# A two-layer diffusion block: where twelve modulation pairs of the first layer are placed, and how much room attention asks for

## The chip, the cores and the metric

The kernel runs on one core of a Trainium2 chip. TensorE (PE) does the matrix products, VectorE (DVE), ScalarE (ACT) and GpSimd (POOL) the elementwise work, and SyncE (SP) issues all DMA transfers from one queue, in order. The metric is the device time of one execution in microseconds (us); lower is better.

## The reference, cut to what matters

The program computes two layers of a block that works on 512 latent tokens and 256 context tokens of width 1024. All values are float32.

```
for i in range(2):
    mod_l = split(silu(c) @ mod_w[i] + mod_b[i], 6)       # six modulation vectors, latent
    mod_c = split(silu(c_ctx) @ mod_w[i] + mod_b[i], 6)   # the same for the context
    h_l = rms_norm(x, g) * (1 + mod_l[1]) + mod_l[0]      # and h_c
    pa, pb, pc, pd = split(h @ w_in[i])                   # projections of four mixers
    o = concat(rwkv7(pa), diff_attention(pb), gla(pc), gqa(pd))
    x = x + mod_l[2] * (o @ w_out[i])
    x = x + mod_l[5] * conv_ffn(modulate(x, g2, mod_l[3], mod_l[4]), ...)
    # the context xc takes the same path in the first layer
```

Parts 0 and 1 of the modulation are needed ahead of the projections. Parts 2, 3 and 4 are needed only when all four mixers are done: part 2 at the output projection, parts 3 and 4 at the norm after it. These three parts are 24 vectors of 128 channels in the first layer, and the kernel works them out in twelve pairs. They are the pairs of this change.

## The kernel before, in words

**Streams on a planned clock.** Each piece of work is a Python generator that issues instructions and then yields a planned duration in planned nanoseconds. `weave` (line 305) keeps a planned clock for each stream and always advances the stream whose clock is lowest; so the yields set the order in which instructions are issued, and no yield is a measured time. An engine takes its instructions in an order close to that one: the framework below may let a few later instructions of the same engine pass while one waits, as the trace shows at the modulation pairs. Below, "plan 192" means 192 thousand planned nanoseconds after the start of a layer's mixing stage.

**The mixing stage** of a layer weaves `rwkv`, `gla`, `attentions` and `projections`, and in the first layer `mod_mix`. `projections` (line 776) multiplies the normed input by eighteen blocks of `w_in`: eleven feature blocks of 7,776 planned ns each in the first layer and seven token blocks of six tiles of 2,640. Each block sets a flag for its consumer: `da ready` comes after eleven feature blocks and five token blocks, `gq ready` after all of them. Then it gives back the input (eight slabs), the weight ring (four) and the staging ring. `attentions` waits for `da ready` and then, in `begin` (line 1074), until a number of whole slabs is free (`room`, line 871). `rwkv` makes features for two directions, two passes each (`front`, line 1517, with `features` from line 1417); each pass waits until nine half slabs and two whole ones are free (`halves`). Direction 0 then inverts small blocks in a long row of VectorE steps (lines 1492 and 1494) and starts its chain of chunks (`rw_prep`, `rw_chain`), each of which asks for seven whole slabs; direction 1 does the same after its own features.

**On-chip buffers** come from an arena of 30 slabs of 1,536 float32 columns, cut into 24 grains of 64. A slab holds one kind of data (plain float32, or the rounded form that the split-precision matmuls read). A buffer that breaks a whole slab pays a price in `find`, and buffers of a third of a slab are put at the thirds.

**A modulation pair** (`mod_pair`, line 465) loads 1 MB of weights, issues eight matmuls of 32 by 256 columns in four column strips (line 470, two recorded passes each), a ScalarE copy out of PSUM (line 472), two small matmuls that sum the strips (line 474) and a VectorE add (line 477). `mod_mix` (line 521) issues the twelve later pairs. It has three buffers of 1,024 columns, loads each pair in two halves of 512 KB, uses the buffers in turn, takes a PSUM bank of the first four, and yields 16,000 after each pair. Attention and the projections use the same four banks.

**Split-precision weights** (`weights`, line 367): each weight tile is loaded to the staging ring (line 376), rounded by ScalarE (line 382), and the rest is taken by GpSimd (line 383); three matmuls per tile follow (lines 392 for features, 770 for tokens). In attention, keys and queries are rotated (lines 917 to 924), split (936, 937), transposed on TensorE (432), and then come scores (1012, 1015), the maximum (1018), the exponential (1020) and the values (1048).

Of the kernel before, what the change touches and what calls it, by code (L numbers as in the profile page):

```python
# [223 lines left out]
class Net:  # L224
# [293 lines left out]
        self.free(first, ms, r, t1, t2, rb, ps)  # L518
        return rs

    def mod_mix(self, dt):

        ws = [self.new([4, 256]) for _ in range(3)]
        e = 0
        for i in range(KD, len(MODP)):
            w = []
            for q in range(2):
                self.nc.sync.dma_start(out=ws[e % 3], in_=self.A["modp"][i][:, 4 * q:4 * q + 4])
                w += [ws[e % 3][:, k] for k in range(4)]
                e += 1  # L530
            ps = yield from self.bank(1, 0, 4)
            self.mod_pair(i, w, ps)
            self.free(ps)
            yield dt
        self.free(*ws, self.c32)
# [425 lines left out]
    def attentions(self, li, S):  # L961
# [10 lines left out]
        def keys(g):  # L972
            hd, nh = g.hd, P // g.hd
            for t in range(NT):
                raw = load(g, "k", t, g.hp * P, P)
                y = self.rope(raw, t, nh, hd, g.ktab, g.C["kr"][:, t, g.hp * nh:g.hp * nh + nh])
                s = self.new([4, P], F32R)
                if g.da:
                    self.split_stack(s.rearrange("p h (c d) -> p h c d", c=4), y, "HLHL", 4, 32)
                else:  # L980
                    sv = s.rearrange("p (e h) (c d) -> p e h c d", e=2, c=2)
                    yb = y.unsqueeze(2).to_broadcast([P, 2, 2, 64])
                    nc.scalar.copy(out=sv[:, 0], in_=yb)
                    nc.vector.tensor_tensor(out=sv[:, 1], in0=yb, in1=sv[:, 0].bitcast(F32), op=ALU.subtract)
                yield from self.transpose4(s, g.kst[t // 3][:, :, t % 3 * P:(t % 3 + 1) * P], 0, self.AB)
                self.free(s, raw)
                yield 1200
# [86 lines left out]
        def begin(kind, hp, before):  # L1074

            g = SimpleNamespace(kind=kind, hp=hp, da=kind == "da", hd=32 if kind == "da" else 64, qs={})
            yield from self.wait(S, kind + " ready")
            if before is None:
                yield from self.room(5)
            g.C = S[kind]  # L1080
            if hp:
                g.ktab, g.qtab, g.nlam, g.lam_init = before.ktab, before.qtab, before.nlam, before.lam_init
            else:
                g.ktab = self.rope_tables(kind, g.hd, self.rw[kind + "k"], 1.0)
                g.qtab = self.rope_tables(kind, g.hd, self.rw[kind + "q"], g.hd ** -0.5)
                if g.da:
                    g.nlam, g.lam_init = self.diff_lambda(li)
            g.kst = [self.new([4, hb], F32R) for _ in range(2)]
            g.vs = self.new([NT, 2, 64])
            nc.sync.dma_start(out=g.vs.rearrange("p t h d -> p t (h d)"),  # L1090
                              in_=self.raws["da", "v"][:, :, hp * P:hp * P + P] if g.da else self.raws["gq", "k"][:, :, P:2 * P])
            yield from keys(g)
            g.oT = [self.new([T]) for _ in range(1 if g.da else 2)]
            g.units = []
            for t in range(nt):
                g.units += [(t, hi) for hi in range(0, 2 if g.da else 4, 2)]
            return g
# [21 lines left out]
        parts = (("da", 0), ("da", 1), ("gq", 0))  # L1119
        ready, late, ends = [], None, []  # L1120
        nxt = yield from begin(*parts[0], None)
        for i in range(len(parts)):
            g = nxt
            for t, hi in g.units:
                if t not in g.qs:
                    yield from self.room(self.ROOM[li][3])
                    yield from queries(g, t)
                for h in (hi, hi + 1):
                    yield from self.room(self.ROOM[li][3])
                    got = yield from scores(g, t, h)  # L1130
                    if late is not None:
                        ready.append(late[:3] + (combine(late[0], *late[3]),))
                    late = (g, t, hi, got)
                    if len(ready) == 2:
                        yield from pair(ready, ends)
                        ready = []
                if (t, hi) == g.units[-1] or g.units[g.units.index((t, hi)) + 1][0] != t:
                    self.free(g.qs.pop(t))
            self.free(*g.kst)
            if i + 1 < len(parts):  # L1140
                yield from self.room(self.ROOM[li][2])
                nxt = yield from begin(*parts[i + 1], g)
            if i + 1 == len(parts) or parts[i + 1][1] == 0:
                self.free(g.ktab[3], g.qtab[3])
# [711 lines left out]
    def run(self):  # L1856
# [28 lines left out]
        def last(li, S):  # L1885
            x, hf, spans = [], [], self.spans(li < L - 1)
            parts, sts = [[q] for q in spans], [{}, {}]
            yield from self.w_out(li, od, xd[li], x, sts)
            yield from self.norm(li, "nfg", x, sts, hf, parts)
            S["normed"] = True  # L1890
            sts = [{}, {}]

            def done(m, i, a, b):
                if li < L - 1:
                    nc.sync.dma_start(out=xd[1][:, m, a:b], in_=x[m][:, a:b])
                    self.squares(x, m, a, b, sts[i])
                else:
                    nc.sync.dma_start(out=self.out[:, m, a:b], in_=x[m][:, a:b])

            yield from self.ffn(li, x, hf, done, S)  # L1900
            if li < L - 1:
                self.rings(4, 3)
                yield from self.norm(li + 1, "nmg", x, sts, h, parts)
            else:
                self.free(*x)
# [4 lines left out]
        for li in range(L):  # L1910
            self.load_rows(li)
            self.arena.BREAK = 100
            self.AB, S = 4, {}
            streams = [self.rwkv(li, S, od), self.gla(li, S, od), self.attentions(li, S), self.projections(li, h, S)]
            if li == 0:
                streams.append(self.mod_mix(16000))
            self.weave(*streams, pace=self.PACE[li][:1] + self.PACE[li][2:])
            self.rings(4, 3)
            h = []
            streams = [last(li, S)]  # L1920
            self.arena.BREAK = 40
            if li < L - 1:
                streams.append(self.ffn_mod(S))
            else:
                S["ffn gate"] = True
            self.weave(*streams)
# [19 lines left out]
```

## Time and profile before

| what | value |
|---|---|
| median of 3 runs | 2382.31 us (2373.57 to 2385.05) |
| the profiled execution | 2371.69 us, its span 2369.8 us |
| mean granted TensorE clock | 0.954 of full speed |
| TensorE busy | 2194.0 us (93%) |
| VectorE busy | 1327.0 us (56%) |
| twelve later pairs, first weights issued | 37.8 us |
| twelve later pairs, last weights issued | 329.6 us |

Busy times say how long an engine had an instruction running; since matmuls overlap and their ends are modelled, a full TensorE row means that it was never without work, not that it ran at its peak. The granted clock is 1.00 at the upper of two levels (2.4 GHz) and 0.50 at the lower one (1.2 GHz), averaged over a stretch. "Idle before" an instruction names the engine whose result it waited for.

### The profile page before, as it was taken

To read this page: it belongs to the slowest core of one execution; us is meant where nothing else is said; L and a number is where in the kernel's file an instruction comes from. 1 tells how busy PE (TensorE), PEld (TensorE's weight loads), DVE (VectorE), ACT (ScalarE), POOL (GpSimd) and SP (SyncE) were. 2 spreads that over 40 slices of the span, in tenths; PEclk is the share of its full clock that TensorE was granted. 3 is DMA by queue.
4 is the path that set the end of the run, shared out by engine and by line. 5 is a ranking of instruction groups with operands and counts; after the bars stand their busy time and mean duration, and the time that the engine had idled before them with its cause. 6 is when DMAs were issued, how large, how long until landed. Compare 5 with 4: busy or idle time off the path is not lost. (4 is left out here: it accounts for less than half of the span.)

```text
span 2369.8 us, 40603 instructions
## 1 busy us (share of the span) xinstructions
PE 2194.0 (93%) x15656; PEld 1852.1 (78%) x15656; DVE 1327.0 (56%) x2900; ACT 934.2 (39%) x1730; POOL 995.9 (42%) x999
## 2 busy tenths in 40 slices
PE   7989996889989999999999989995899979999999
PEld 3877786768768788888888877785778868888888
DVE  3143567878864696765445643378877565332323
ACT  3333222555564422322223443332465544433333
POOL 1433437123422344434434634455443224555556
PEclk7999997889999999999999989997889989999999
DMA  8322354433234243343333521144233242333334
GB/s 324 116 72 82 102 150 108 105 89 93 58 123 143 82 137 116 109 142 106 116 107 107 172 65 55 59 126 132 69 98 87 77 138 72 102 94 99 98 98 134
DMA packets 241265, 258.51 MB, mean 109 GB/s; under 512 B 102896, under 2 KB 186160, under 8 KB 241072
## 3 DMA queue, kind: packets, MB, share of 16 engines
q1 hardware_dynamic: 241072, 255.92, 36.1%
q8 instruction: 123, 2.02, 0.4%
q14 instruction: 70, 0.57, 0.1%
HBM read 209.69 MB, written 37.77 MB: 104 GB/s over the span
## 5 line engine op out<-in xcount | busy, mean ns | idle before, releaser
L392 PE MATMUL pst<-slab,slab 128*128 128x512 f32 (+1 forms) x6552 | 1236.5, 350 | 14.4 <-POOL slab L650 5.8
L392 PEld LDWEIGHTS pst<-slab,slab 128*128 128x128 f32 x6552 | 1049.6, 190 | 195.8 <-issue 11.3
L383 POOL TENSOR_TENSOR slab<-slab,slab 128x512 fp32r<-128x512 f32 (+1 forms) x428 | 563.7, 1326 | 661.1 <-ACT slab L382 621.3
L382 ACT CAST slab<-slab 128x512 fp32r<-128x512 f32 (+1 forms) x428 | 258.7, 612 | 592.3 <-PE pst L392 418.6
L770 PE MATMUL pst<-slab,slab 128*128 128x256 f32 (+1 forms) x1872 | 254.1, 295 | 9.3 <-POOL slab L383 8.0
L770 PEld LDWEIGHTS pst<-slab,slab 128*128 128x128 f32 x1872 | 242.4, 199 | 20.4 <-POOL slab L383 9.5
L432 PE MATMUL pst<-cst,slab 128*128 128x128 f32 (+1 forms) x968 | 166.4, 305 | 69.1 <-DVE slab L937 21.7
L683 DVE SCALAR_TENSOR_TENSOR slab<-pst,pp,slab 128x511 f32<-128x511 f32 x66 | 41.6, 658 | 299.2 <-ACT slab L680 299.2
L432 PEld LDWEIGHTS pst<-cst,slab 128*128 128x128 f32 (+1 forms) x968 | 120.6, 153 | 96.6 <-DVE slab L937 24.3
L1620 PE MATMUL pst<-slab,slab 128*128 128x128 f32 (+4 forms) x1320 | 160.8, 283 | 7.3 <-DVE slab L1646 3.4
L1620 PEld LDWEIGHTS pst<-slab,slab 128*128 128x128 f32 (+3 forms) x1320 | 132.3, 179 | 29.6 <-issue 14.6
L714 DVE SCALAR_TENSOR_TENSOR slab<-pst,fgate,slab 128x512 f32<-128x512 f32 (+1 forms) x144 | 88.2, 628 | 104.9 <-PE pst L392 104.7
L1020 ACT ACTIVATE slab<-pst,mx 128x768 f32<-128x768 f32 (+1 forms) x120 | 97.7, 815 | 67.6 <-DVE mx L1018 64.3
L1018 DVE TENSOR_REDUCE mx<-pst 128x1 f32<-128x768 f32 (+1 forms) x120 | 100.2, 846 | 35.6 <-PE pst L1012 20.1
L695 POOL TENSOR_TENSOR slab<-slab,slab 128x768 fp32r<-128x768 f32 (+1 forms) x44 | 73.9, 1680 | 70.2 <-ACT slab L694 70.2
L551 DVE SCALAR_TENSOR_TENSOR slab<-slab,slab 128x512 bf16<-128x512 f32 x104 | 92.2, 886 | 5.1 <-DMA slab<-in_modw_dram 3.5
L1048 PE MATMUL pst<-slab,slab 128*64 128x128 f32 x832 | 67.0, 290 | 5.0 <-DVE slab L429 2.9
L1031 ACT ACTIVATE slab<-slab,r 128x768 f32<-128x768 f32 (+1 forms) x80 | 67.7, 852 | 10.0 <-DVE r L1030 9.3
L689 ACT ACTIVATE slab<-slab 128x768 f32<-128x768 f32 (+1 forms) x44 | 32.4, 737 | 85.7 <-DVE slab L685 85.6
L694 ACT CAST slab<-slab 128x768 fp32r<-128x768 f32 (+1 forms) x44 | 32.1, 729 | 85.0 <-DVE slab L691 84.9
L1012 PE MATMUL pst<-slab,slab 128*128 128x384 f32 (+1 forms) x144 | 48.8, 407 | 14.0 <-ACT slab L1020 6.4
L1048 PEld LDWEIGHTS pst<-slab,slab 128*64 128x64 f32 x832 | 46.9, 141 | 18.1 <-DVE slab L429 6.3
(320 smaller groups left out, 2626.6 us busy)
## 6 DMA issues: line engine op xcount, KB each, us to landing
slab<-in_wup_dram SPq DMA_DIRECT2D x88, 512.0 KB, 3.7
slab<-in_modw_dram SPq DMA_DIRECT2D x112, 256.0 KB, 3.0
slab<-in_wdn_dram SPq DMA_DIRECT2D x48, 512.0 KB, 3.5
slab<-in_win_dram SPq DMA_DIRECT2D x46, 512.0 KB, 3.9
slab<-in_modp_dram SPq DMA_DIRECT2D x40, 512.0 KB, 7.0
slab<-in_wout_dram SPq DMA_DIRECT2D x16, 512.0 KB, 3.7
slab<-in_xT_dram SPq DMA_DIRECT2D x16, 384.0 KB, 5.3
slab<-kb SPq DMA_DIRECT2D x24, 256.0 KB, 3.0
```

The costliest lines, as they stand in the source:

```text
L382: nc.scalar.copy(out=w[0], in_=st[:, k:k + q])
L383: nc.gpsimd.tensor_tensor(out=w[1], in0=st[:, k:k + q], in1=w[0].bitcast(F32), op=ALU.subtract)
L392: self.nc.tensor.matmul(ps[:, a:b], w[i][k][:, cols], x[j][k][:, a:b], start=(k == 0 and q == 0), stop=(k == nk - 1 and q == 2))
L432: self.nc.tensor.transpose(out, a.bitcast(F32) if a.dtype != F32 else a, self.c["ident"])
L551: self.tc.keep_in_program_order(nc.vector.scalar_tensor_tensor(out=junk, in0=w, scalar=1.0, in1=self.sc[s][e], op0=ALU.mult, op1=ALU.mult, ...
L695: nc.gpsimd.tensor_tensor(out=HL[:, 1, :n], in0=th[:, :n], in1=HL[:, 0, :n].bitcast(F32), op=ALU.subtract)
L714: nc.vector.scalar_tensor_tensor(out=x[m][:, a:b], in0=ps[:, a:b], scalar=gate[:, m, s:s + 1], in1=x[m][:, a:b], op0=ALU.mult, op1=ALU.add)
L770: self.nc.tensor.matmul(ps[:, :n], h[i][k][:, t * P:(t + 1) * P], w[j][k], start=(k == 0 and q == 0), stop=(k == KD - 1 and q == 2))
L1018: nc.vector.tensor_reduce(out=mx, in_=sv, axis=AX.XY, op=ALU.max, negate=True)
L1020: nc.scalar.activation(out=p[m][:, a:].rearrange("p (e c) -> p e c", e=2 - a // hb), in_=sv, func=AF.Exp, bias=mx, accum_out=lsum[:, m:m + 1])
L1048: nc.tensor.matmul(acc[64 * e:64 * e + 64, :P], vs[e][:, i + j], aT[:, 256 * j + P * e:256 * j + P * e + P], start=(first and j == 0), sto ...
L1620: mm = lambda o, a, b, pos: nc.tensor.matmul(o, a, b, start=True, stop=True, tile_position=pos)
```

## The change

`mod_mix` waits for the flag `gq ready`, which the projections set after their last block. It takes twelve buffers of 512 columns (a third of a slab each, four slabs in all) in place of three of 1,024. A pair's weights come in four DMAs of 256 KB in place of two of 512 KB, so 48 in all in place of 24, and three pairs fit in the buffers at once. After each pair it yields 4,000 in place of 16,000. The buffer `c32`, which holds the condition vector, stays in use until the last pair, as before. Attention's first `begin` of a layer asks for six whole slabs in place of five; this holds in both layers. The pairs themselves, `mod_pair`, are as they were.

```
-    def mod_mix(self, dt):
+    def mod_mix(self, S, dt):
-        ws = [self.new([4, 256]) for _ in range(3)]
-        e = 0
+        n = 12
+        yield from self.wait(S, "gq ready")
+        ws = [self.new([2, 256]) for _ in range(n)]
         for i in range(KD, len(MODP)):
             w = []
-            for q in range(2):
-                self.nc.sync.dma_start(out=ws[e % 3], in_=self.A["modp"][i][:, 4 * q:4 * q + 4])
-                w += [ws[e % 3][:, k] for k in range(4)]
-                e += 1
+            for q in range(4):
+                t = ws[(4 * i + q) % n]
+                self.nc.sync.dma_start(out=t, in_=self.A["modp"][i][:, 2 * q:2 * q + 2])
+                w += [t[:, k] for k in range(2)]
             ps = yield from self.bank(1, 0, 4)
             self.mod_pair(i, w, ps)
             self.free(ps)
...
             if before is None:
-                yield from self.room(5)
+                yield from self.room(6)
...
             if li == 0:
-                streams.append(self.mod_mix(16000))
+                streams.append(self.mod_mix(S, 4000))
```

## Rows read from the trace of the kernel before

**Rows 1.** The page's first part: TensorE's busy time, share of the span, instructions.
```profile
PE 2194.0 (93%) x15656; PEld 1852.1 (78%) x15656; DVE 1327.0 (56%) x2900; ACT 934.2 (39%) x1730; POOL 995.9 (42%) x999
```

**Rows 2.** Windows (us): length, busy us per engine, clock, DMA share, GB/s.
```profile
80.00:340.00 260.00, 246.42 (x2128) 211.25 (x2127) 100.38 (x219) 79.19 (x138) 106.60 (x100) 0.96 0.35 107
340.00:440.00 100.00, 76.48 (x612) 65.03 (x611) 80.83 (x190) 32.81 (x66) 47.34 (x68) 0.83 0.38 98
440.00:560.00 120.00, 105.21 (x930) 85.85 (x930) 93.82 (x236) 66.48 (x145) 33.22 (x62) 0.89 0.36 91
560.00:680.00 120.00, 110.48 (x1123) 91.40 (x1123) 98.25 (x294) 64.45 (x143) 45.70 (x76) 0.95 0.27 73
...
1600.00:1680.00 80.00, 48.69 (x319) 43.87 (x318) 67.52 (x179) 25.01 (x50) 37.02 (x60) 0.74 0.38 105
```

**Rows 3.** Timeline of TensorE after the projections: start, length, line, [idle before].
```profile
390.74 1.11 PE L432 MATMUL pst<-cst,slab 128*128 128x128 f32 x4 [4.86 <-DVE slab L937]
397.08 3.03 PE L432 MATMUL pst<-cst,slab 128*128 128x128 f32 x13 [3.41 <-DVE slab L937]
410.29 3.61 PE L1620 MATMUL pst<-slab,slab 128*64 128x128 f32 x24 [3.01 <-DVE slab L1646]
...
726.19 24.12 PE L392 MATMUL pst<-slab,slab 128*128 128x512 f32 x131
```

**Rows 4.** Timeline of TensorE round one modulation pair.
```profile
308.87 1.07 PE L470 MATMUL pst<-slab,slab 128*32 128x256 f32 x16
309.87 0.74 PE L770 MATMUL pst<-slab,slab 128*128 128x256 f32 x4
310.44 0.59 PE L474 MATMUL pst<-cst,slab 128*128 128x2 f32 x4
310.90 2.63 PE L770 MATMUL pst<-slab,slab 128*128 128x256 f32 x20
```

**Rows 5.** Timeline at the two pairs that stalled TensorE.
```profile
283.64 1.02 PE L474 MATMUL pst<-cst,slab 128*128 128x2 f32 x4 [2.91 <-ACT slab L472]
355.48 0.84 ACT L1430 ACTIVATE slab<-slab 128x768 f32<-128x768 f32 x1 [6.58 <-DVE slab L1428]
356.90 1.02 PE L474 MATMUL pst<-cst,slab 128*128 128x2 f32 x4 [4.27 <-ACT slab L472]
```

**Rows 6.** Waits: SP's queue to 345 us, TensorE over the span (total us, times, longest).
```profile
SPq L528 <- PE pst L470: 35.4, 9, 9.6
...
PE pst L770 <- POOL slab L383: 8.0, 6, 3.0
```

**Rows 7.** Timeline of TensorE: rwkv's feature matmuls, first layer, then second.
```profile
297.27 2.85 PE L1424 MATMUL pst<-slab,lora 64*128 64x512 f32 x8
...
345.07 2.85 PE L1424 MATMUL pst<-slab,lora 64*128 64x512 f32 x8
...
1563.83 2.85 PE L1424 MATMUL pst<-slab,lora 64*128 64x512 f32 x8
...
1579.72 2.84 PE L1424 MATMUL pst<-slab,lora 64*128 64x512 f32 x8
```

**Rows 8.** Windows, VectorE alone: length, busy us, clock, DMA share, GB/s.
```profile
299.70:310.40 10.70, 7.43 (x8) 1.00 0.67 201
311.60:327.50 15.90, 1.67 (x6) 1.00 0.92 256
```

**Rows 9.** Waits of TensorE for ScalarE over the span: total us, times, longest.
```profile
PE pst L432 <- ACT slab L1020: 11.3, 16, 2.3
PE pst L474 <- ACT slab L472: 10.8, 10, 4.3
```

**Rows 10.** DMA issues (count, KB each, us to landing); a window of all engines.
```profile
slab<-in_modw_dram SPq DMA_DIRECT2D x112, 256.0 KB, 3.0
...
slab<-in_modp_dram SPq DMA_DIRECT2D x40, 512.0 KB, 7.0
...
20.00:40.00 20.00, 16.17 (x110) 8.09 (x111) 8.69 (x24) 5.17 (x12) 5.16 (x4) 0.51 1.03 405
```

## The prediction

> **What bounds the kernel now.** I read the page first: TensorE is busy for 93% of the span [rows 1], so the question is where it is not. The windows by stage answer that [rows 2]. From 80 to 340 us, in the first layer's projections, TensorE is busy 246.4 of 260 us, while VectorE has 100.4 and GpSimd 106.6: this stretch is bound by TensorE, and whatever leaves its queue there shortens it. From 340 to 440 us, where the projections end and attention and rwkv start, TensorE is idle for 23.5 of 100 us at a granted clock of 0.83, and VectorE is busy for 80.8. From 440 to 560 us it is idle for 14.8 of 120 us, VectorE at 93.8; from 560 to 680 us for 9.5. So the mixers' stretch is a chain over several engines, with VectorE the fullest. The timeline shows the same in single gaps: TensorE sits idle 4.86, 3.41 and 3.01 us for VectorE's results at 391, 397 and 410 us [rows 3]. The next stage's matmuls start at 726 us [rows 3]; attention is the last mixer before it.
>
> **The pairs leave the projections.** One pair costs TensorE 1.00 us for the eight strip matmuls (308.87 to 309.87) and 0.46 us for the sums (310.44 to 310.90), 1.46 us in all; other matmuls fill the time of the copy [rows 4]. Two of the twelve pairs run ahead of 80 us, where TensorE also waits for the norm; I give those nothing. Ten pairs by 1.46 us are 14.6 us. Two pairs stalled TensorE, because ScalarE's copy came late: 2.91 us and 4.27 us [rows 5]. In the second case ScalarE itself had stood 6.58 us behind a VectorE scan. These 7.2 us go with the pairs. What is late next is the projections' own weights, for which TensorE waited 8.0 us over the whole run in six waits [rows 6]; so I take 5.0 of the 7.2 (bounds 0 and 7.2). SP's queue stood 35.4 us before the twelve pairs' loads, since a buffer was still being read [rows 6]; weights queue behind them. They arrived in time all the same, so I take nothing for it (at most the 8.0 us of TensorE's waits for weights, which cover both layers). Sum of the removal: -19.6 us.
>
> **The pairs come into the mixers' stretch.** Twelve pairs by 1.46 us are 17.5 us of TensorE's time. By the yields of the code the projections end at plan 196 (eleven blocks of 7,776 and 42 tiles of 2,640), and the pairs take 48 from there. Attention's last yield falls at plan 392. The last 196 of the plan take from 386 us (390.74 less 4.86) to 726 us [rows 3], 1.73 us each, so the pairs are spread over some 83 us from the projections' end on. That stretch has TensorE idle for 38.3 of 220 us (340 to 560). Each pair also makes TensorE, which runs its queue in order, wait for ScalarE's copy; behind the waiting matmuls are scores, transposes and rwkv's blocks, and VectorE and ScalarE wait for those. The trace of before has one pair in this stretch, the last, and it waited 4.27 us [rows 5]. The nearest wait of the same engines that is met often there, a transpose behind an exponential, is 11.3 us in 16 waits, 0.7 us each; the pairs' own waits were 10.8 us in 10, with a longest of 4.3 [rows 9]. I take the common wait, 0.7 us, since the one pair stood behind a scan that ends with the features: twelve waits add 8.4 us. Bounds: nothing, if all of it falls into idle time, and 12 x (1.46 + 4.27) = 69 us, if each pair waits like the worst and nothing hides it. Work that TensorE gets into its gaps is free, work ahead of a chain step is not; with 17% of TensorE's time idle here and VectorE at 79%, I take half of 17.5 + 8.4 us: +13.0 us. The pair's one short copy on ScalarE and one short add on VectorE lie in this.
>
> **The loads.** Twelve pairs bring 12 x 1.05 MB. SP issues 24 more DMAs. The first twelve need buffers that the projections gave back, so SP may stand there until the last weights are rounded; behind it are attention's and rwkv's loads, for which there is no row, between nothing and the 35.4 us that SP stood at such loads before [rows 6]. After that a load of pair i+3 waits for pair i's matmuls, and what is queued behind it is used after pair i anyway: I take nothing, the pairs being three deep. Traffic from 340 to 440 us is 98 GB/s [rows 2]; the most that a stretch shows is 405 GB/s [rows 10]. The difference, 307 GB/s, loads a pair in 3.4 us, against 4 plan units or 6.9 us from pair to pair: the loads keep up, at no cost.
>
> In the trace a 256 KB load lands after 3.0 us and one of 512 KB after 7.0 us [rows 10], so here the smaller one is not dearer by the byte. The Trainium skill (DMA: Bandwidth & Descriptors, section Bandwidth) asks for transfers of at least 1 MiB for three quarters of the peak, and its section Anatomy of one DMA puts a constant of about 2.0 us on each. An estimate by that page: 24 more transfers by 2.0 us are 48 us, which would be paid only one after another.
>
> **What the three buffers free.** Until the projections end, `mod_mix` holds no slab any more; its three buffers had each taken two thirds of one. In the first layer the features' third pass follows the second after 47.8 us (297.27 to 345.07), in the second layer, which has no such pairs, after 15.9 us (1563.83 to 1579.72) [rows 7]. The pass asks for nine halves; with three more whole slabs, six halves, it can start right behind the second pass, some 30 us earlier. VectorE's work for a pass is 7.43 us in eight instructions; and from 311.6 to 327.5 us VectorE is busy for only 1.67 of 15.9 us [rows 8]. So one pass goes wholly into idle time, and the fourth, which follows it, in part. Both leave the stretch where TensorE waits for VectorE. I take 1.5 passes: -11.1 us; bounds 0 (other VectorE work is late in their place) and -14.9 us (both passes). The second layer speaks for care: there the passes come early, and yet TensorE is idle for 31.3 of 80 us from 1600 us on [rows 2].
>
> **Six slabs.** In the plan attention may start at 164.7 (`da ready`), but in the kernel before its five slabs come free only when `mod_mix` ends, at 192 of the projections' 196.4. Now six must be free, and the third and fourth pass compete for them. If they come only with the projections' end, attention starts 4.4 plan units or 7.6 us later; if the passes end early, it starts up to 10 units or 17 us sooner. I take 0 between these ends. In the second layer six slabs are free by the allocator's count when five are asked for, so I expect no change there.
>
> **The sum.** -19.6 + 13.0 - 11.1 = -17.7 us. Against the profiled execution (2369.8 us of span, 1.9 us round it, 2371.7 us) that is 2354 us. This execution was 10.6 us under the median of the runs shown, 2382.3 us; applied to the median the sum gives 2364.6, and I predict 2364 us, or 0.8% less.
>
> **Rivals.** (B) All fits into gaps: the pairs cost nothing, both stalls and both passes count: -14.6 - 7.2 - 14.9 = -36.7, 2346 us. For it: 38.3 us of idle time in the right place. Against it: TensorE's queue is in order, and its gaps are not where the pairs stand. (C) Paid back: the passes' place is taken by other VectorE work, and the pairs' 17.5 us lie in full on the chain: -19.6 + 17.5 = -2, 2380 us. For it: the second layer's 31.3 us. (D) Slower: every pair holds TensorE for ScalarE's copy, because ScalarE stands behind VectorE's maximum, as at 356.9 us. At 2.91 us, the smaller of the two stalls [rows 5], with nothing hidden: 12 x 4.37 = 52.4 us, less 30.7, +22, 2404 us. It decides from 30.7/12 = 2.6 us per pair on the chain. For it: one PSUM bank of attention's four is held meanwhile. Against it: of the pairs' ten waits, the other eight share 3.6 us. (E) The loads come one behind the other: 4 x 3.0 = 12 us a pair, 5.1 us over the 6.9 that it has; TensorE waits for each: 12 x (1.46 + 5.1) - 30.7 = +48, 2430 us. That is what the page's constant would make of it; twelve buffers in flight speak against it. (F) The six slabs come late, and the change does not let attention start sooner: -17.7 + 7.6 = -10, 2372 us.
>
> **How the numbers follow.** Forecast 38%, B 17%, C 22%, D 13%, E 3%, F 7%. A measurement of this kernel tells about 0.5% from no change, 12 us: faster means under 2370, slower over 2394 us. Faster: 34% of the forecast's 38, B's 17, 2 of C and 3 of F, 56%. Same: 4 of the forecast, 19 of C, 4 of F, 2 of D, 29%. Slower: 1 of C, 11 of D, E's 3, 15%. The forecast's own range is 2353 to 2375 us. For 8 in 10 the range reaches into B to 2342 and into D to 2400 us.
>
> **What would show it.** No line 470 between 80 us and the projections' end, and the projections' last matmuls (before: done at 386 us) some 20 us earlier; the third group of line 1424 close behind the second; twelve pairs in the 83 us after the projections, with waits of line 474 for line 472 under 1 us (over 2.6 us each: D); less idle time after the projections and a higher granted clock there; no waits of line 470 for its loads (E). If the projections shorten and the stretch up to the output projection grows by as much, C is right.

## The result, and the profile after

The changed kernel takes 2396.91 us (median of 5 runs, 2392.24 to 2407.45); the kernel before takes 2380.74 us in the same comparison. The ratio is 1.0083, with a 95% interval from 1.0055 to 1.0111: slower by 13 to 26 us. The forecast was 2364 us. The profiled execution of the changed kernel took 2396.91 us, its span 2395.1 us, 25.3 us more than the profiled execution before.

In the changed kernel, lines behind `mod_mix` have a number that is higher by one (770 is now 771). The page's first line of busy times and the windows of the same stretches as in [rows 1, 2]:

```profile
PE 2200.2 (92%) x15656; PEld 1852.8 (77%) x15656; DVE 1337.9 (56%) x2900; ACT 934.4 (39%) x1730; POOL 1005.8 (42%) x999
```

```profile
80.00:340.00 260.00, 236.18 (x2038) 205.20 (x2036) 124.48 (x263) 83.40 (x140) 120.37 (x111) 0.96 0.28 83
340.00:440.00 100.00, 74.94 (x571) 60.91 (x571) 75.07 (x203) 32.69 (x70) 38.23 (x59) 0.79 0.46 129
440.00:560.00 120.00, 107.21 (x1026) 82.97 (x1025) 72.98 (x178) 60.45 (x137) 28.81 (x55) 0.96 0.51 141
560.00:680.00 120.00, 111.89 (x1164) 93.68 (x1163) 93.86 (x266) 62.19 (x140) 44.89 (x78) 0.96 0.25 65
1600.00:1680.00 80.00, 52.87 (x443) 47.70 (x442) 58.19 (x132) 17.68 (x38) 38.26 (x48) 0.78 0.51 132
```

VectorE's work has moved: 124.5 us in the projections (100.4 before), 73.0 us between 440 and 560 us (93.8 before). But TensorE's 246.4 us in the projections' window became 236.2 us. With the pairs gone, the matmuls behind them should have moved up and kept it full; instead it ran dry. The timeline of TensorE shows where, behind the four groups of rwkv's feature matmuls (line 1425, as in [rows 7]):

```profile
249.73 2.85 PE L1425 MATMUL pst<-slab,lora 64*128 64x512 f32 x8
276.01 2.85 PE L1425 MATMUL pst<-slab,lora 64*128 64x512 f32 x8
294.41 2.84 PE L1425 MATMUL pst<-slab,lora 64*128 64x512 f32 x8
318.60 2.84 PE L1425 MATMUL pst<-slab,lora 64*128 64x512 f32 x8
...
340.71 1.56 PE L1466 MATMUL pst<-slab,slab 64*64 64x64 f32 x48 [13.20 <-DVE slab L1444]
350.70 4.86 PE L1548 MATMUL pst<-rk,slab 128*128 128x2 f32 x22 [8.43 <-POOL slab L1455]
359.02 3.16 PE L432 MATMUL pst<-cst,slab 128*128 128x128 f32 x12 [3.46 <-DVE slab L938]
361.83 0.56 PE L771 MATMUL pst<-slab,slab 128*128 128x256 f32 x1
...
731.43 0.62 PE L392 MATMUL pst<-slab,slab 128*128 128x512 f32 x2 [0.78 <-ACT slab L1811]
```

The third pass follows the second after 18.4 us (47.8 before), about as forecast. Then the blocks of the fourth pass, the bonus and attention's first transposes stand in TensorE's queue ahead of the projections' last block, and TensorE waits 25 us for VectorE and GpSimd. The projections' last matmul ends at 395 us (386 before); the output projection starts at 731.4 us (726.2 before). The pairs stand between 395 and 511 us, and the waits that the prediction spoke of are small. Waits of TensorE and of SP's queue over the whole span, and the DMA issues:

```profile
PE pst L474 <- ACT slab L472: 3.5, 7, 0.5
PE pst L470 <- DMA slab<-in_modp_dram: 1.8, 3, 1.2
...
SPq L530 <- PE pst L1548: 7.6, 1, 7.6
SPq L530 <- PE pst L470: 5.9, 2, 5.7
...
slab<-in_modp_dram SPq DMA_DIRECT2D x48, 256.0 KB, 4.1
```

All of the 3.5 us and 1.2 of the 1.8 us lie before 80 us, at the eight pairs of the first parts, which use the same lines and which the change leaves alone. From 395 to 731 us line 474 has no wait on TensorE's row, and line 470 has these:

```profile
PE pst L470 <- ACT slab L1021: 2.2, 1, 2.2
PE pst L470 <- DMA slab<-in_modp_dram: 0.6, 2, 0.5
```

In the second layer, where no pair stands and the change only asks for a sixth slab, TensorE's timeline has rwkv's chunks (line 1621) first, and attention's first scores (line 1013) only 44 us later; before, the scores came first (second fence, the kernel before):

```profile
1646.75 1.16 PE L1621 MATMUL pst<-slab,slab 64*128 64x64 f32 x16
...
1690.56 0.62 PE L1013 MATMUL pst<-slab,slab 128*128 128x384 f32 x2
```

```profile
1656.90 0.97 PE L1012 MATMUL pst<-slab,slab 128*128 128x384 f32 x4 [0.73 <-ACT slab L427]
...
1660.75 1.97 PE L1620 MATMUL pst<-slab 64*128 64x64 f32 x8
```

From the second layer's first projection matmul of a token block (line 771) to its first output-projection matmul the trace has 590.2 us (568.8 before). So of the 25.3 us, 5.2 lie in the first layer up to the output projection, 21.4 in this stretch, and -1.3 in the rest.

### The profile page after: what moved, and what is told of

Same layout as the page of the kernel before. It is cut to its first block, busy times and chain, and to the rows that moved or that the text cites. A ratio compares the mean times of both kernels' runs of the same rounds, so it can differ in the third digit from the quotient of the medians.

```text
span 2395.1 us, 40625 instructions
## 1 busy us (share of the span) xinstructions
PE 2200.2 (92%) x15656; PEld 1852.8 (77%) x15656; DVE 1337.9 (56%) x2900; ACT 934.4 (39%) x1730; POOL 1005.8 (42%) x999
## 5 line engine op out<-in xcount | busy, mean ns | idle before, releaser
L392 PEld LDWEIGHTS pst<-slab,slab 128*128 128x128 f32 x6552 | 1048.3, 190 | 193.7 <-POOL slab L651 10.1
L771 PE MATMUL pst<-slab,slab 128*128 128x256 f32 (+1 forms) x1872 | 260.1, 298 | 27.7 <-POOL slab L383 15.4
L432 PE MATMUL pst<-cst,slab 128*128 128x128 f32 (+1 forms) x968 | 160.9, 298 | 59.5 <-DMA slab<-ra 12.9
L552 DVE SCALAR_TENSOR_TENSOR slab<-slab,slab 128x512 bf16<-128x512 f32 x152 | 137.0, 902 | 4.9 <-DMA slab<-in_modw_dram 2.8
L1021 ACT ACTIVATE slab<-pst,mx 128x768 f32<-128x768 f32 (+1 forms) x120 | 97.8, 816 | 69.1 <-DVE mx L1019 55.7
L1708 POOL TENSOR_TENSOR slab<-cst,pcu 64x256 f32<-64x256 f32 x48 | 30.9, 645 | 77.5 <-PE pst L1739 19.0
## 6 DMA issues: line engine op xcount, KB each, us to landing
slab<-in_modp_dram SPq DMA_DIRECT2D x16, 512.0 KB, 10.1
```

What stands on the lines that cost most here:

```text
L392: self.nc.tensor.matmul(ps[:, a:b], w[i][k][:, cols], x[j][k][:, a:b], start=(k == 0 and q == 0), stop=(k == nk - 1 and q == 2))
L432: self.nc.tensor.transpose(out, a.bitcast(F32) if a.dtype != F32 else a, self.c["ident"])
L552: self.tc.keep_in_program_order(nc.vector.scalar_tensor_tensor(out=junk, in0=w, scalar=1.0, in1=self.sc[s][e], op0=ALU.mult, op1=ALU.mult, ...
L771: self.nc.tensor.matmul(ps[:, :n], h[i][k][:, t * P:(t + 1) * P], w[j][k], start=(k == 0 and q == 0), stop=(k == KD - 1 and q == 2))
L1021: nc.scalar.activation(out=p[m][:, a:].rearrange("p (e c) -> p e c", e=2 - a // hb), in_=sv, func=AF.Exp, bias=mx, accum_out=lsum[:, m:m + 1])
```

## The experiments

All times come with a ratio to the kernel before on the same chip. "Output projection" is the start of the first layer's output projection in the profiled execution, "second layer" the stretch just defined. How far such a number can be trusted: the kernel before, e15 and e16 issue the same first layer, and reached the output projection at 726.2, 722.2 and 731.0 us; the changed kernel and e1 at 731.4 and 739.5. A difference under 9 us in it is not told apart by one profile each; the changed kernel's 5.2 us is such a difference. e3, e5, e7, e8 and e9 leave the twelve pairs' matmuls out, with constants in their place, and e6 loads weights for three pairs only: these runs price parts of the work and are no candidates.

**First: which part costs?** e1 pins the second layer's order; e2 moves the pairs but nothing else in the first layer; e3 has no pairs; e4 holds the third pass back.

```
# e1: the changed kernel, and
                 yield from self.room(6)
+                S["att in"] = True
...
+            if li:
+                yield from self.wait(S, "att in")
             yield from self.room(self.ROOM[li][1])
# e2: e1, and in mod_mix
+        held = [self.new([4, 256]) for _ in range(3)]
+        yield 192000
+        self.free(*held)
         yield from self.wait(S, "gq ready")
# e3: the kernel before, mod_mix reduced to
         ws = [self.new([4, 256]) for _ in range(3)]
+        yield 12 * dt
         self.free(*ws, self.c32)
# e4: e1, and in direction
             if d:
+                if not li:
+                    yield from self.wait(S, "gq ready")
                 yield from front(1)
```

> The changed kernel with one line more: in the second layer rwkv's first direction asks for its seven slabs only after attention's first begin has its room (a flag). The first layer is issued as in the changed kernel. Theory 1 (of the 16 us lost, some 20 us lie in the second layer, because other slabs are free there and rwkv passes attention in the plan): first attention scores of the second layer again about 27 us ahead of where the changed kernel has them, first output-projection matmul about 20 us earlier against the first layer's, time 2374 to 2380 us. Rival 1 (the twelve pairs hold TensorE among the mixers, nothing is wrong in the second layer): no change, 2393 to 2400 us.

e1: 2388.18 us, ratio 1.0059 (1.0037 to 1.0080). The second layer came out 578.9 us long, 11.3 less than in the changed kernel and 10.1 more than before; half of theory 1's 20 us. The two ratios' intervals overlap, so the totals of e1 and the changed kernel are not told apart.

> As e1, and mod_mix holds three buffers of 1,024 columns up to plan 192 without using them, as before the change, so that the features' third and fourth pass and attention come at the planned time of the kernel before; only the pairs are moved. Theory 1 with theory 2 (the early passes put rwkv's matmuls, which wait for VectorE, ahead of the projections' last blocks): projections' last matmul at 366 to 372 us (386 before, 395 after), time 2362 to 2372 us, below e1 by 5 to 15. Rival 1 (pairs cost among the mixers what they gave back): 2378 to 2390 us. Rival 2 (the early passes are a gain, as predicted): e2 slower than e1 by about 11 us.

e2: 2422.17 us, ratio 1.0198 (1.0177 to 1.0219), which none of the theories had. The projections' last matmul ended at 366.4 us, as theory 2 said; but the output projection started at 758.9 us, 32.7 later than before.

> The kernel before with the twelve later pairs left out (loads, matmuls, copies; constants stand in their place), its three buffers held as long as before. It prices what the pairs cost where they were. The prediction's term: 19.6 us by ten pairs and two stalls, 21 to 25 us with the first two pairs and all of the stalls, so 2356 to 2361 us. Rival (that stretch is bound by VectorE behind TensorE, so the time comes back): 2375 to 2381 us.

e3: 2346.74 us, ratio 0.9881 (0.9865 to 0.9897). The projections end at 364.2 us, the output projection starts at 703.2: 21.6 and 23.0 us earlier than before. The term of 19.6 us stands; the rival falls.

> As e1, and in the first layer the second direction's features (third and fourth pass) wait for the flag that the projections' last block sets; the slabs are free, attention may take them. Theory 2: projections' last matmul at 366 to 372 us, no idle time of 13 and 8 us on TensorE behind VectorE and GpSimd before it; the passes then stand in the mixers' stretch. Time 2365 to 2376 us, below e1 by up to 10. Rival 2 (early passes are a gain): slower than e1 by 5 to 15 us, since two passes of 7.4 us VectorE time come where VectorE is fullest.

e4: 2435.20 us, ratio 1.0257 (1.0237 to 1.0277). The projections end at 370.1 us, but the output projection starts at 767.4. Theory 2 saw only half: with the pairs in place, early passes are not what makes the changed kernel slow.

**Second: e2 less e3 is 55.7 us in the first layer. What are they?** Parts of e2 alone, and the changed kernel without pairs.

```
# e5: e2 with no pairs, loads only
-            ps = yield from self.bank(1, 0, 4)
-            self.mod_pair(i, w, ps)
-            self.free(ps)
# e6: e2 with 12 loads
+                if i < KD + 3:
                     self.nc.sync.dma_start(out=t, in_=self.A["modp"][i][:, 2 * q:2 * q + 2])
# e7: e2, after the twelve buffers are taken only
+        yield 12 * dt
# e8: e1, mod_mix reduced to
         yield from self.wait(S, "gq ready")
+        yield 12 * dt
         self.free(self.c32)
```

> As e2, but of the twelve pairs only the 48 loads are left (no matmuls, copies, sums; constants stand in their place); they keep their planned places. e2 stands 75 us above e3, which has neither loads nor pairs. Theory 3 (the loads take SyncE's in-order queue and the DMA engines from rwkv's and attention's small transfers, which land later): 2385 to 2415 us, most of the 75. Theory 4 (rival D: the pairs' matmuls hold TensorE for ScalarE's copy): 2347 to 2360 us.

e5: 2389.10 us, ratio 1.0072 (1.0050 to 1.0094), output projection at 729.0 us.

> As e2, with all twelve pairs' matmuls, copies and sums, but only the first three pairs load weights (12 loads in place of 48); the others multiply by what lies in the buffers. Theory 3 (loads): 2365 to 2390 us. Theory 4 (TensorE held by pairs): 2405 to 2422 us.

e6: 2392.92 us, ratio 1.0078 (1.0049 to 1.0107), output projection at 733.4 us.

> As e2, with no loads and no pairs (constants in their place): twelve buffers are only held from the projections' end to plan 244.6. Theories 3 and 4: 2345 to 2355 us, as e3. Theory 5 (four slabs held in the mixers' stretch keep rwkv and attention from their buffers): 2380 to 2420 us.

e7: 2360.81 us, ratio 0.9942 (0.9921 to 0.9964), output projection at 703.1 us. Holding four slabs costs the first layer nothing. But e7's second layer is 580.4 us long and e3's 567.0, with attention first in both. e7 asks for six slabs there and e3 for five; e9 below asks for six too and takes 570.4, so the places of the buffers are the likelier cause of the 13 us.

So loads alone cost 729.0 - 703.1 = 25.9 us, pairs with a quarter of the loads 30.3, both together 55.8. Neither theory 3 nor theory 4 is the whole. Theory 4's mechanism falls: waits of line 474 for line 472 are 0.4 us in e6 and none in e2 in this stretch. What TensorE does pay is the matmuls themselves. Groups of the two lines, count | busy us, mean ns | idle before: first the kernel before, where ten pairs stand from 80 to 360 us; then the changed kernel and e2, twelve pairs, from the projections' end to the output projection:

```profile
L470 PE MATMUL pst<-slab,slab 128*32 128x256 f32 x160 | 11.9, 386 | 0.0
L474 PE MATMUL pst<-cst,slab 128*128 128x2 f32 x40 | 6.5, 268 | 7.2 <-ACT slab L472 7.2
```

```profile
L470 PE MATMUL pst<-slab,slab 128*32 128x256 f32 x192 | 20.3, 429 | 2.8 <-ACT slab L1021 2.2 <-DMA slab<-in_modp_dram 0.6
L474 PE MATMUL pst<-cst,slab 128*128 128x2 f32 x48 | 7.6, 262 | 0.0
```

```profile
L470 PE MATMUL pst<-slab,slab 128*32 128x256 f32 x192 | 26.9, 510 | 2.7 <-ACT slab L1024 2.4 <-DVE slab L429 0.2
L474 PE MATMUL pst<-cst,slab 128*128 128x2 f32 x48 | 8.4, 279 | 0.0
```

Twelve pairs are 35.3 us of TensorE's row in e2 and 27.9 in the changed kernel. By the same measure ten pairs were 18.4 us before, so twelve would be 22.1; the 17.5 of the prediction goes from start to start [rows 4]. In e2's windows of 366 to 440 and 440 to 520 us the granted clock is 0.75 and 0.81, between its levels of 1.2 and 2.4 GHz. In e3, without pairs, it is 0.77 and 0.87 there, so most of that is not the pairs' doing. How much of e6's 30.3 us this is was not tried.

What the loads do is seen in SP's queue. Its timeline (start, length, line), first in e7, then in e5; line 1500 (1504 in e5) loads the keys of rwkv's chunks:

```profile
360.02 1.89 SPq L1500 DMA_DIRECT2D slab<-kb  x2
...
424.58 0.58 SPq L1500 DMA_DIRECT2D slab<-kb  x1
...
431.00 0.60 SPq L1500 DMA_DIRECT2D slab<-kb  x1
```

```profile
417.60 2.01 SPq L533 DMA_DIRECT2D slab<-in_modp_dram  x4
419.65 0.43 SPq L1504 DMA_DIRECT2D slab<-kb  x1
...
426.87 3.99 SPq L533 DMA_DIRECT2D slab<-in_modp_dram  x8
430.97 1.37 SPq L1690 DMA_DIRECT2D slab<-slab  x2
432.39 4.02 SPq L533 DMA_DIRECT2D slab<-in_modp_dram  x4
...
443.31 2.01 SPq L533 DMA_DIRECT2D slab<-in_modp_dram  x4
445.37 0.43 SPq L1504 DMA_DIRECT2D slab<-kb  x1
```

From 417.6 to 445.4 us SP spends 12.0 of 27.8 us on pairs' loads, in bursts between the mixers' small transfers. The third chunk's load, which e7 issues with the second at 360 us, goes out at 419.65 us in e5, and GpSimd stands for it (waits of GpSimd in e5, 365 to 729 us):

```profile
POOL slab L1655 <- DMA slab<-kb: 36.7, 1, 36.7
```

In e3, without any pairs' loads, that load went out at 404.61 us, and GpSimd waited 2.9 us in all for such loads, so a late issue alone is not the price. Which of the late transfers decides is not settled; e11 below tests the queue itself.

> As e1 (the changed kernel with attention first in the second layer), with the twelve later pairs left out: no loads, no matmuls, no buffers (constants in their place). Prices the pairs in the mixers' stretch of the changed kernel itself. The prediction's +13.0 would make it 2375 us against e1's 2388; the price by e2 less e3 in the first layer (some 53 us) would make it 2330 to 2345 us.

e8: 2387.74 us, ratio 1.0054 (1.0037 to 1.0071), output projection at 719.2 us. This was the surprise of the study: with no pairs at all (and attention first in the second layer) the changed kernel is still slower than the kernel before with them, and no faster than e1. In the first layer the pairs cost the changed kernel 12.2 us (731.4 less 719.2) or 20.3 (e1's 739.5); the price of e2 does not carry over. That the total is no better lies in e8's second layer: 593.9 us, 15.0 more than e1's, with the same code and attention first in both.

**Third: is it the passes or attention's start, and what are the loads' bytes worth?**

```
# e9: e8; e10: e1; both with, in begin and in mod_mix,
+                if not li:
+                    yield from self.wait(S, "att go")
                 yield from self.room(6)
...
+        yield 192000
+        S["att go"] = True
         yield from self.wait(S, "gq ready")
# e11: e2 with
-                self.nc.sync.dma_start(out=t, ...)
+                self.nc.scalar.dma_start(out=t, ...)
# e12: e2 with four buffers [4, 256] and, as before the change, two loads of 512 KB a pair
```

> As e8 (changed kernel, attention first in the second layer, no pairs), but attention's first begin of the first layer waits until plan 192, where it started before the change. So only the features' third and fourth pass come early. In the first layer e8's output projection started 16 us behind that of e3, which has no pairs either and the memory as before (719.2 against 703.2 us). Theory 6 (the early passes do it: their chain stands on VectorE and GpSimd ahead of the projections' last blocks): output projection at 715 to 722 us, last projection matmul at 390 to 400. Theory 7 (attention's early start does it): output projection at 700 to 706 us, last projection matmul at 362 to 370, time 2345 to 2362 us.

e9: 2364.01 us, ratio 0.9957 (0.9939 to 0.9975); the projections end at 384.8 us, the output projection starts at 715.4, 12.2 us later than e3's. Early passes alone do most of the 16 us (the rest, 3.8 us, is within what profiles differ by); theory 6 holds, though the projections end some 5 us sooner than it said. What waits, in TensorE's timeline of e9, is the projections' own weights, whose rest GpSimd takes late:

```profile
338.96 2.10 PE L763 MATMUL pst<-slab,slab 128*128 128x256 f32 x13 [3.87 <-ACT slab L845]
355.73 1.65 PE L763 MATMUL pst<-slab,slab 128*128 128x256 f32 x6 [14.66 <-POOL slab L383]
```

> As e9, with the twelve pairs among the mixers as in the changed kernel. Against e2 only the passes are earlier, against e1 only attention is later. e2's output projection started at 758.9, e1's at 739.5 us. Theory 6: 735 to 745 us (the passes do all of it). Theory 7: the pairs then cost what they cost in e2, some 53 us over e9.

e10: 2410.44 us, ratio 1.0158 (1.0126 to 1.0189), output projection at 752.6 us. The pairs cost 37.2 us over e9; against e2 it is 6.3 us earlier, within what profiles differ by, and attention's early start (e1) gives another 13.1. Neither theory's numbers came.

> As e2, with the 48 loads issued from ScalarE's DMA queue in place of SyncE's. The loads alone made the first layer 26 us longer (e5 less e7). Theory 3a (they fill SyncE's in-order queue, where the small transfers of rwkv and attention stand behind them): 2394 to 2408 us, most of the 26 comes back. Theory 3b (the bytes themselves delay the small transfers in the DMA engines): 2415 to 2430 us; ScalarE's own work waits for 48 issues besides.

e11: 2384.16 us, ratio 1.0040 (1.0020 to 1.0059), output projection at 725.2 us, 33.7 earlier than e2's. Theory 3a holds: the same bytes from another queue are far cheaper. The small transfers are not faster for it: 64 KB loads from `scrout` land after a median of 3.7 us in e11 as in e2 (2.4 in e3). The line's own answer in e2, then in e11 (duration of an issue in ns, min/median/max, and the landing in us):

```profile
L533 SPq DMA_DIRECT2D slab<-in_modp_dram x48: 328/429/1457, 361.7 to 499.0; - x48
...
DMA to landing us min/median/max: 2.5/4.1/7.3
```

```profile
L533 ACTq DMA_DIRECT2D slab<-in_modp_dram x48: 334/336/697, 339.4 to 485.6; - x48
...
DMA to landing us min/median/max: 2.5/3.3/5.8
```

The Trainium skill (Trainium Kernel Development and Optimization, section Key Constraints) says that queues of different engines share the same DMA engines, and that issuing from several saves only the issue time. The trace has 48 x 0.429 = 20.6 us of issue on SP, an estimate by the median; the eleven bursts in which SP issues the loads, with its waits inside them, sum to 30.5 us. The saving of 33.7 us is 13 us above the first and 3 us above the second. It is not told apart from the time that the loads hold SP, and so does not contradict the page.

> As e2, with the pairs' weights in 24 loads of 512 KB in place of 48 of 256 KB, in four buffers of 1,024 columns. Theory 3a (SyncE's queue): half of the issues, 2405 to 2415 us. Theory 3b (bytes): 2416 to 2430 us.

e12: 2411.06 us, ratio 1.0155 (1.0138 to 1.0172), output projection at 751.8 us, 7.1 earlier than e2's. The time lies in theory 3a's range, the 7.1 us within what profiles differ by: half of the issues is at best a small part of it.

**Fourth: the changed kernel itself, and the second layer.**

```
# e13: the changed kernel with nc.scalar.dma_start as in e11
# e14: e11 with
-        n = 12
+        n = 6
-                streams.append(self.mod_mix(S, 4000))
+                streams.append(self.mod_mix(S, 9000))
# e15 (e16): the kernel before, with range(3) (range(1))
             self.AB, S = 4, {}
+            if li:
+                self.free(*[self.new([T]) for _ in range(3)])
```

> The changed kernel with one edit: the pairs' 48 loads go out from ScalarE's DMA queue in place of SyncE's. In the changed kernel the pairs cost 20 us of the first layer (e1 less e8), where e2's cost 56, 34 of which the other queue gave back (e11). If SyncE's queue is the price here too: output projection of the first layer 10 to 20 us earlier than the changed kernel's 731 to 739 us, 2380 to 2390 us. If the changed kernel's first layer is held by the early passes and attention alone: within 4 us of it, 2393 to 2400 us. The second layer stays some 590 us long in both.

e13: 2387.41 us, ratio 1.0058 (1.0026 to 1.0089), output projection at 727.8 us, second layer 588.0. That is 4 to 12 us earlier, and the interval overlaps the changed kernel's: not told apart.

> As e11 (memory as before, loads from ScalarE's queue), with six buffers of 512 columns in place of twelve and 9,000 planned ns after each pair in place of 4,000, so that the pairs lie over the whole half of the mixers' stretch. e11's first layer reached the output projection at 725.2 us, e3's without pairs at 703.2. If the pairs' price is their density in the stretch where TensorE's clock is low (366 to 500 us): 712 to 720 us, 2362 to 2378 us. If it is their TensorE time wherever they stand: 722 to 728 us, 2376 to 2388 us.

e14: 2367.46 us, ratio 0.9988 (0.9971 to 1.0005), output projection at 713.5 us, second layer 573.6: as fast as the kernel before, not measurably faster. It differs from e11 in two things, the buffers and the spacing.

> The kernel before, with nothing of the change; at the second layer's start three slabs are taken and at once given back, which issues no instruction and changes only the order in which the allocator hands slabs out. In the plan rwkv's first direction then finds its seven slabs ahead of attention's start, as in the changed kernel. Theory 1 (slab order, not the change's work, costs the second layer its 21 us): second layer (first projection matmul to output projection) 580 to 592 us long in place of 568.8, time 10 to 24 us over the kernel before. Rival: the second layer of the changed kernel suffers from something else, within 4 us of the kernel before.

e15: 2383.93 us, ratio 1.0045 (1.0031 to 1.0060). The second layer is 579.3 us long, 10.5 more than before. TensorE's timeline has the changed kernel's order, chunks first:

```profile
1636.06 1.16 PE L1620 MATMUL pst<-slab,slab 64*128 64x64 f32 x16
...
1670.34 0.69 PE L1012 MATMUL pst<-slab,slab 128*128 128x384 f32 x1 [0.73 <-ACT slab L427]
```

So 0.45%, 10.7 us, is lost by three slabs taken and given back, without an instruction added. Another order of free slabs can make half of the second layer's loss; that far theory 1 holds. e15 changes two things at once, though, the places of the buffers and the order of issue, and does not tell which of them costs.

> As e15, with one slab taken and given back: other slabs are handed out, but the plan keeps its order (attention starts at the same planned time as before). Runs with that order had a second layer of 567 to 570 us or of 579 to 588 us. If the place of the buffers alone makes that difference: any of these, a change of up to 15 us; if only the order of the plan counts: within 3 us of the kernel before.

e16: 2374.15 us, ratio 1.0007 (0.9989 to 1.0026), second layer 568.9 us. Other places for the buffers need not cost anything. But they can, with attention first all the same: the fourteen runs that hold rwkv back until attention has its room (e1, e2, e4 to e12, e14, e17, e18) have the same code in the second layer, and it took from 570.4 us (e9) to 592.3 (e4) and 593.9 (e8), as long as the changed kernel's. The span of 579 to 588 us in the text above left these two out. So attention's place in the order is not shown to be what costs.

**Last: a kernel below both?**

```
# e17: e14 with three buffers [4, 256] and two loads of 512 KB a pair
# e18: e14 with
-                streams.append(self.mod_mix(S, 9000))
+                streams.append(self.mod_mix(S, 12000))
```

> As e14 (memory as before, loads from ScalarE's queue, 9,000 planned ns after each pair), with 24 loads of 512 KB in three buffers of 1,024 columns in place of 48 of 256 KB in six of 512. Half of the issues leave ScalarE's queue, 5 to 15 us of its time. If they stood on the path: output projection of the first layer at 705 to 712 us, 2355 to 2366 us in all, below both kernels. If not: 711 to 716 us, and the time follows the second layer (567 to 588 us long), 2362 to 2385 us.

e17: 2386.97 us, ratio 1.0061 (1.0042 to 1.0080), output projection at 736.4 us, second layer 575.0.

> As e14, with 12,000 planned ns after each pair in place of 9,000, so that the pairs reach over three quarters of the mixers' stretch. If density is the price: output projection at 706 to 712 us, 2355 to 2366 us. If the price is TensorE's time: 712 to 718 us, as e14, 2362 to 2385 us by the second layer's length.

e18: 2389.85 us, ratio 1.0074 (1.0051 to 1.0098), output projection at 723.5 us, second layer 585.8. Both are slower than e14, though each was to help: neither the issues nor the density is shown to be the price, and e14's place is not explained. No version of this study that works out the pairs beats the kernel before.

The first layer's output projection, by where the pairs stand and what is early:

| | no pairs | pairs among the mixers |
|---|---|---|
| memory as before | 703.2 (e3), 703.1 (e7) | 758.9 (e2) |
| passes early | 715.4 (e9) | 752.6 (e10) |
| passes and attention early | 719.2 (e8) | 731.4 (changed), 739.5 (e1) |

The kernel before, with its pairs in the projections: 726.2.

## Why the prediction was wrong, step by step

- **The pairs leave the projections, -19.6 us: right.** e3 shows -21.6 at the projections' end and -23.0 at the output projection. With the memory as before the projections did end 19.5 us earlier (e2); in the changed kernel they ended 9 us later, because of the freed buffers (below).
- **The pairs among the mixers, +13.0 us: too small.** They cost 12 to 20 us in the changed kernel and, with their loads, 56 where nothing else moves. The waits for ScalarE's copy, 8.4 us in the working, were none on TensorE's row from 395 to 731 us. The working had read the row for them wrongly: of the ten waits [rows 9] the eight that share 3.6 us lie before 80 us, at the pairs of the first parts, so of the twelve later pairs all but two had none. TensorE's time, 17.5 us in the working (22.1 by the measure of the groups above), measured 27.9 to 35.3. "I take half" had no row under it; only the changed kernel's stretch, with 73.0 us of VectorE work from 440 to 560 us in place of 93.8, comes near it.
- **The loads, nothing: wrong** with the memory as before: 25.9 us (e5). I had looked for TensorE waiting for weights, and it hardly did. The price lay in SP's queue (e11); which of the transfers behind the loads decides stays open. I had written "I take nothing, the pairs being three deep".
- **What the three buffers free, -11.1 us: the sign was wrong without pairs and right with them.** "So one pass goes wholly into idle time": VectorE was idle, but the pass also issues matmuls, and TensorE's queue is in order. GpSimd and VectorE then came late for what stood in it. e9 and e8, without pairs, show +12.2 and +16.0 us by the output projection. With pairs the freed memory gained 19.4 to 27.5 us (e2 against e1 and the changed kernel), more than the forecast. The row that spoke for care, the second layer's early passes with TensorE idle for 31.3 of 80 us [rows 2], was quoted and left out of the sum.
- **Six slabs, no change in the second layer: wrong by 21.4 us.** The count that I took was the kernel before's. Moved buffers leave the slabs in another order, and in the plan rwkv's first direction gets its seven ahead of attention. e15 shows 10.5 us of loss from another order of free slabs alone, and e1, with attention first, takes 11.3 off. Whether the order of issue or the places of the buffers cost it is not settled, nor are the remaining 10 us: with attention first, equal code took 570.4 to 593.9 us. The sixth slab need not cost: e9 asks for it and took 570.4. No run moves the pairs and keeps five slabs.

The sum by the profiled executions, from the kernel before over e3 and e8: -23.0 + 16.0 + 12.2 in the first layer, +21.4 in the second, -1.3 in the rest, 25.3 us, against -17.7. Two steps failed. The pairs among the mixers, their loads and the freed buffers were put at 13.0 + 0 - 11.1 = +1.9 us together; they measured +28.2 (36.3 by e1's profile). And the second layer, put at nothing, measured +21.4. How the first of these divides depends on the order: by e3 and e8 the freed buffers' -11.1 is off by 27.1 us and the pairs' +13.0 is nearly right (12.2); by e3 and e2, the order of the prediction's own sum, the pairs and loads are 55.7 in place of 13.0 and the freed buffers gain 27.5. For the terms don't add: from e3, pairs alone cost 55.7 us and the freed memory 16.0, and both together 28.2 to 36.3, not 71.7. That one part of the sum came near its measured value on one of these ways is luck. Why early work makes the pairs so much cheaper was not tried; that VectorE then has less to do among the mixers is argued only.

Of the rivals, D named the size for the memory as before (52.4 us against 55.8) by a mechanism that is not there. E falls: among the mixers TensorE waited 0.6 us for the loads. The estimate of 48 us for 24 more transfers went by the constant of the Trainium skill (DMA: Bandwidth & Descriptors, section Anatomy of one DMA), which that section gives for transfers issued from GpSimd; these went out from SyncE, and with 24 loads fewer e12 came only 7.1 us earlier than e2. C, "paid back", came nearest for the first layer: -23.0 us and +28.2 leave 5.2, which one profile each does not tell from nothing.

## What to carry to other kernels

Price a moved step on every in-order queue that it passes, the DMA queue too: 48 loads that nothing read cost 26 us (e5). When a change gives buffers back early, ask what starts with them and whose queue that fills, and replay the allocator in every later stage: three slabs taken and given back cost 10.7 us in a layer where not one instruction was added (e15). Where two edits fill the same idle time, a sum of their separate prices is not a forecast.

## What the runs showed of the hardware

- While the pairs' loads were under way, 64 KB transfers took a median of 3.7 us to land (loads from `scrout` from 366 to 520 us in e2), against 2.4 in e3 from 364 to 500 us. With the loads in ScalarE's queue it was 3.7 as well (e11, 365 to 520 us), though the stage was 33.7 us shorter: those 33.7 us were not the price of the later landing.
- One small DMA can cost SP more time than one large load: a median of 0.608 us for the issue of a 64 KB load of e2's line 1513, 0.429 for a 256 KB load of line 533.
